# Which engine issues the loads of the context's raw weights: SyncE or GpSimd

## The chip, the cores and the metric

One core of one Trainium2 chip runs the whole program. The metric is the device time of one execution in microseconds (us). Below, PE is TensorE's matmuls, PEld its weight loads, DVE VectorE, ACT ScalarE, POOL GpSimd, SP SyncE; SPq and POOLq are the queues on which SP and POOL issue their DMAs.

## What is computed

Two transformer blocks, one after the other, on 256 tokens of width 1024, all in float32. The first has two attentions, a cross attention and a mixture of 32 experts (two chosen per token). The second is two layers deep and runs on two sequences: the tokens that leave the first block, and a context of 256 rows that depends on no token. The part that matters here is the context's, which in the first layer goes through an FFN, a mixer and another FFN, and in the second layer through one more FFN and a key and value projection:

```
mod = silu(c) @ ada_w + ada_b                    # 9 vectors of 1024 for each layer
h  = h + 0.5 * mod[2] * swiglu(modulate(h, mod[0], mod[1]), w_in, w_out)
swiglu(h) = (silu(g) * u) @ w_out,   g, u = split(h @ w_in),   hidden width 2816
```

All of the context's work can run beside the first block. Its result is needed only in the second layer's attention of the tokens.

## The kernel before

A float32 weight is read from DRAM as a "raw" tile and is split into two float32r parts: a high part, which ACT copies (`sph`), and a low part, raw minus high (`spl`). Each product is then three matmuls (high by high, high by low, low by high). `split` does this for pieces of 128 x 512.

There are two streams of work with buffers of their own, class `Stream`. `fore` (its tiles are named f...) has the first block, the experts and the tokens; its raw tiles are 128 x 2048 (1024 KB), five buffers. `back` (tiles b...) has the context; its raw tiles are 128 x 1024 (512 KB), five buffers, and three buffers each for `bsph` and `bspl`. In `back` the low part is subtracted by POOL (`LOW`, line 32: b=(1, 1)), in `fore` by DVE, with few exceptions.

- `load` (lines 182 to 185) takes a raw tile and issues its DMA on SP, for both streams. `pair` (187) calls it once for a wide tile and twice for a narrow one. The context's weights come through it: 132 tiles of `ffn_in`, 66 of `ffn_out`, 32 of the mixer (`e_sv`, `e_qk`, `e_u`, `e_v`, `e_o`, `e_out`) and 4 of `o_k` and `o_v`, 234 in all, and so 468 subtractions on POOL.
- `ada` (528) loads the modulation weights for `back` straight on SP, partly into the same raw buffers; PE reads those tiles itself. `narrow` (599) and the table of the spatial gate (1400 to 1402) also load on SP.
- `experts_in` and `experts_out` (1155 to 1184) load 24 wide tiles for each of 8 groups of experts, and multiply them directly, in float32, with no split.
- `squares` (264) adds squares of the residual, with POOL in two of its steps (278).
- `out_proj` (359), `ffn_steps` (419) and `even_steps` (1320) call these in turn.

Order: a planner lays out each engine's instructions once, when the program is built, by a priority that each stream works out from a due time (`SEG`, line 1797, and `priority`, 86): a start plus a slope times the matmul work that the stream has done. On the chip every engine then takes its instructions in that fixed order. `link` (157) adds edges for the planner: an instruction comes after the one before it of the same stream on the same engine key, and `self.after` can add one more edge. These edges are of the kind NoSync: they bind the planner's order, and put no wait into the program. The splits have a chain of their own (`S.side`, line 200), so the planner may put them anywhere between the loads of their engine.

At the loop for left-over experts (lines 1267 to 1274) the first stretch ends. Three of the six rounds of the context's last FFN are meant for before it (`PLAN`, -1: 'rrr'), three for after. Line 1912 says that the first SP instruction of the late rounds comes after `K.moe_load`, the last load of an expert weight.

Of the kernel before, what the change touches and what calls it, by code (L numbers as in the profile page):

```python
# [69 lines left out]
class Stream:  # L70
# [18 lines left out]
    def low(self, nc):  # L89

        self.lows += 1
        return nc.gpsimd if self.pool_low and self.lows % self.pool_low[1] < self.pool_low[0] else nc.vector

    def t(self, tag, shape, dt=F32):
        self.n += 1
        return self.pool.tile(shape, dt, tag=tag, bufs=self.bufs[tag], name=f"{self.name}{tag}{self.n}")
# [52 lines left out]
class Kern:  # L149
# [31 lines left out]

    def load(self, S, src):
        raw = S.t("raw", [128, S.unit])
        self.nc.sync.dma_start(raw, src)
        return raw

    def pair(self, S, src):
# [6 lines left out]
    def misc(self, S, tag, shape, src, dt=F32):  # L194
        t = S.t(tag, shape, dt)
        self.real.gpsimd.dma_start(t, src)
        return t
# [39 lines left out]
    def newton(self, S, src, n, scale, eps):  # L237
        nc = self.nc
        v, y, t = S.t("c", [128, n]), S.t("c", [128, n]), S.t("c", [128, n])
        nc.vector.tensor_scalar(v, src, scale, eps, op0=OP.mult, op1=OP.add)  # L240
        nc.vector.tensor_scalar(t.bitcast(I32), v.bitcast(I32), 1, None, op0=OP.arith_shift_right)
        nc.vector.tensor_scalar(y.bitcast(I32), t.bitcast(I32), -1.0, float(0x5F3759DF), op0=OP.mult, op1=OP.add)
        for _ in range(3):
            nc.vector.scalar_tensor_tensor(t, y, -0.5, y, op0=OP.mult, op1=OP.mult)
            nc.vector.tensor_tensor(t, t, v, op=OP.mult)
            nc.vector.scalar_tensor_tensor(y, t, 1.5, y, op0=OP.add, op1=OP.mult)
        return y
# [1554 lines left out]
def kernel(ctx: ExitStack, tc: tile.TileContext, I, out, dbg=None, stop=None):  # L1802
    K = Kern(tc, I, dbg)
    nc = K.nc
# [39 lines left out]
    def late(what):  # L1844
        c = K.cres
        for w in what:
            if w == "r":
                next(K.c1a)
            elif w == "a":
                m = K.nada  # L1850
                K.nada += 1
                for _ in K.ada(back, 1, range(m, m + 1), ("raw",)):
                    pass
            elif w == "k":
                assert next(K.c1a, None) is None and K.nada >= 5
                if dbg:
                    dbg("hc1a", c)
                K.odd_kv(back, K.modulated(back, c, 1, 3, 1))
# [49 lines left out]
    for i in range(PLAN_N):  # L1908
        if i in PLAN:
            K.cur, K.stream = back.chain, back  # L1910
            if i == 0:
                K.after["sync"] = K.moe_load
                back.seg(*SEG["c1a"])
            elif "tensor" in fore.chain:
                K.after["tensor"] = fore.chain["tensor"]
            late(PLAN[i])
        K.cur, K.stream = fore.chain, fore
        if i == 0:
            fore.seg(*SEG["tok"])
        next(steps, None)  # L1920
# [154 lines left out]
```

## Time and profile before

| | |
|---|---|
| median of 3 runs | 2590.99 us (2584.66 to 2596.36) |
| the profiled execution | 2586.39 us, of which the span of instructions is 2584.6 us |
| PE busy | 2391.1 us, 93% of the span |
| POOL busy | 732.7 us, 28% |
| DMA moved | 617.37 MB, 239 GB/s over the span |

The profile is one execution. Its share of busy time is a mean over unlike stages: the start (to some 236 us), the first block with the first pieces of the context (to 452), experts and context together (452 to 1232), experts alone (1232 to 1320), and the tokens (to the end, with the last context work between 1320 and 1765). The rows of the stages stand below. A matmul record that lasts longer than its share of PE's time overlaps its neighbours, so busy PE is read as "something was running".

### The profile page before, as it was taken

The page shows a single profiled execution, that of the slowest core. Times are in us where ns is not written, and L with a number is a line of the kernel's source. Part 1 is how long each engine was busy: PE and PEld are TensorE (multiplying, and loading weights), DVE is VectorE, ACT ScalarE, POOL GpSimd, SP SyncE. Part 2 cuts the span into 40 slices and gives each one's busy share as a digit, 9 for nine tenths or more (in the row PEclk, how much of TensorE's full clock was granted, in tenths as well). Part 3 has the DMA queues.
Part 4 walks back from the last instruction along what each step waited for, and adds up shares of the span by engine and source line. Part 5 has one row for each costly group of instructions (what it writes and reads, how often), then busy time and mean ns, then how long its engine had stood idle before and what let it go on. Part 6 is the DMA issues. An engine that isn't in the chain of part 4 may idle for free. (4 is left out here: it accounts for less than half of the span.)

```text
span 2584.6 us, 48422 instructions
## 1 busy us (share of the span) xinstructions
PE 2391.1 (93%) x19032; PEld 2066.7 (80%) x19032; DVE 1482.6 (57%) x3179; ACT 1185.6 (46%) x2342; POOL 732.7 (28%) x584
## 2 busy tenths in 40 slices
PE   6999998998988999999679999998999899889998
PEld 4767998786666888878259998988899899767998
DVE  6555767335434334252147676766767866677766
ACT  4433554334433433444035555545555555465554
POOL 1000145664524665756041004231000100424000
PEclk9999999999989999999789999998999999899999
DMA  9897543997989898988874554462455455355452
GB/s 375 298 338 266 178 139 109 377 353 280 388 303 347 341 347 302 367 322 339 330 299 169 188 188 136 173 209 83 156 187 181 151 190 182 112 199 196 172 188 98
DMA packets 115238, 617.37 MB, mean 239 GB/s; under 512 B 13232, under 2 KB 14704, under 8 KB 63936
## 3 DMA queue, kind: packets, MB, share of 16 engines
q1 hardware_dynamic: 113616, 610.20, 64.2%
q0 software_dynamic: 1392, 4.06, 0.5%
q8 instruction: 150, 2.46, 0.4%
q14 instruction: 80, 0.66, 0.1%
HBM read 612.11 MB, written 2.10 MB: 238 GB/s over the span
## 5 line engine op out<-in xcount | busy, mean ns | idle before, releaser
L58 POOL TENSOR_TENSOR bspl<-braw,bsph 128x512 fp32r<-128x512 f32 x468 | 611.2, 1315 | 885.9 <-ACT bsph L58 757.8
L58 ACT ACTIVATE fsph<-fraw 128x512 fp32r<-128x512 f32 x764 | 478.6, 628 | 518.7 <-PE fps L58 438.1
L58 DVE TENSOR_TENSOR fspl<-fraw,fsph 128x512 fp32r<-128x512 f32 x712 | 500.7, 706 | 288.7 <-ACT fsph L58 286.1
L58 PE MATMUL fps<-fxh,fspl 128*128 128x256 f32 (+1 forms) x2000 | 573.4, 287 | 3.5 <-POOL fspl L58 2.5
L58 PE MATMUL fps<-fxh,fsph 128*128 128x256 f32 (+1 forms) x2000 | 574.0, 287 | 2.7 <-ACT fxh L58 2.4
L58 PE MATMUL fps<-fxl,fsph 128*128 128x256 f32 (+1 forms) x2000 | 569.5, 285 | 7.3 <-DVE fxl L58 7.3
L58 ACT ACTIVATE bsph<-braw 128x512 fp32r<-128x512 f32 x468 | 290.7, 629 | 394.4 <-PE bps L58 323.4
L58 PEld LDWEIGHTS fps<-fxl,fsph 128*128 128x128 f32 x2000 | 382.6, 191 | 11.8 <-DVE fxl L58 11.1
L58 PEld LDWEIGHTS fps<-fxh,fsph 128*128 128x128 f32 x2000 | 382.8, 191 | 10.3 <-issue 4.6
L58 PEld LDWEIGHTS fps<-fxh,fspl 128*128 128x128 f32 x2000 | 381.6, 191 | 11.0 <-DVE fspl L58 4.8
L58 PE MATMUL bps<-bxh,bsph 128*128 128x256 f32 x1264 | 365.8, 289 | 10.8 <-ACT bsph L58 5.0
L58 PE MATMUL bps<-bxh,bspl 128*128 128x256 f32 x1264 | 366.4, 290 | 2.8 <-POOL bspl L58 2.3
L58 PE MATMUL bps<-bxl,bsph 128*128 128x256 f32 x1264 | 361.9, 286 | 0.9 <-DVE bxl L58 0.7
L58 PE MATMUL fps<-fk,fsph 128*128 128x256 f32 x1632 | 299.6, 284 | 2.2 <-ACT fk L58 1.5
L58 PEld LDWEIGHTS bps<-bxh,bsph 128*128 128x128 f32 x1264 | 245.4, 194 | 33.0 <-issue 10.2
L58 PEld LDWEIGHTS bps<-bxh,bspl 128*128 128x128 f32 x1264 | 245.4, 194 | 27.2 <-POOL bspl L58 17.7
L58 PEld LDWEIGHTS fps<-fk,fsph 128*128 128x128 f32 x1632 | 255.1, 192 | 7.0 <-DVE fk L58 3.4
L58 PEld LDWEIGHTS bps<-bxl,bsph 128*128 128x128 f32 x1264 | 245.2, 194 | 7.6 <-DVE bxl L58 4.0
L58 PE MATMUL fps<-fraw,fk 128*32 128x512 f32 (+1 forms) x1600 | 213.9, 651 | 37.0 <-DMA fraw<-in_w_eu_dram 20.3
L58 POOL TENSOR_TENSOR fk<-fk,fk 128x512 f32<-128x512 f32 x16 | 21.1, 1322 | 794.0 <-ACT fk L58 788.9
L58 PE MATMUL fps<-fk,fspl 128*128 128x256 f32 x816 | 231.7, 284 | 0.0
L58 DVE SCALAR_TENSOR_TENSOR bk<-bk,bps 128x256 f32<-128x256 f32 (+1 forms) x148 | 60.5, 411 | 250.9 <-ACT bk L58 249.0
(359 smaller groups left out, 3489.7 us busy)
## 6 DMA issues: line engine op xcount, KB each, us to landing
fraw<-in_ffn_in_dram SPq DMA_DIRECT2D x88, 1024.0 KB, 4.9
braw<-in_ffn_in_dram SPq DMA_DIRECT2D x132, 512.0 KB, 6.4
fraw<-in_w_eg_dram SPq DMA_DIRECT2D x66, 1024.0 KB, 7.4
fraw<-in_w_eu_dram SPq DMA_DIRECT2D x66, 1024.0 KB, 9.0
fraw<-in_w_ed_dram SPq DMA_DIRECT2D x66, 1024.0 KB, 7.4
fraw<-in_ffn_out_dram SPq DMA_DIRECT2D x44, 1024.0 KB, 4.9
braw<-in_ffn_out_dram SPq DMA_DIRECT2D x66, 512.0 KB, 5.9
braw<-in_ada_w_dram SPq DMA_DIRECT2D x59, 512.0 KB, 7.4
```

The source lines that it names most:

```text
L58: r = f(*args, **kw)
```

## The change

The loads that go through `load` are issued by POOL for the context's stream, and by SP as before for the other. The edge for the late rounds is hung on the first instruction of the key "gpsimd" instead of "sync", still after `K.moe_load`, which remains an instruction of SP. `ada`, `narrow` and the gate's table stay with SP. The loads of the context are now linked in one chain with the context's other POOL instructions that are not splits, the additions in `squares`.

```diff
+    def loader(self, nc):
+
+        return nc.gpsimd if self.name == "b" else nc.sync
...
     def load(self, S, src):
         raw = S.t("raw", [128, S.unit])
-        self.nc.sync.dma_start(raw, src)
+        S.loader(self.nc).dma_start(raw, src)
         return raw
...
             if i == 0:
-                K.after["sync"] = K.moe_load
+                K.after["gpsimd"] = K.moe_load
                 back.seg(*SEG["c1a"])
```

## Rows read from the trace of the kernel before

**Rows 1.** Page, part 1: busy time, share, instructions.
```profile
PE 2391.1 (93%) x19032; PEld 2066.7 (80%) x19032; DVE 1482.6 (57%) x3179; ACT 1185.6 (46%) x2342; POOL 732.7 (28%) x584
```

**Rows 2.** Stretch, us; busy us of PE, PEld, DVE, ACT, POOL; PEclk; DMA share; GB/s.
```profile
452.00:1232.00 780.00, 742.12 (x5797) 588.42 (x5796) 303.88 (x671) 312.87 (x599) 441.95 (x347) 0.97 0.89 339
1232.00:1320.00 88.00, 51.82 (x301) 15.18 (x300) 8.80 (x20) 4.93 (x9) 3.91 (x4) 0.75 0.90 344
...
646.00:711.00 65.00, 59.89 (x453) 43.87 (x446) 30.39 (x80) 28.77 (x60) 32.46 (x27) 1.00 0.98 387
```

**Rows 3.** PE by group, 1232 to 1320: busy, mean ns, idle before, releasers.
```profile
L58 PE MATMUL fps<-fraw,fk 128*32 128x512 f32 x240 | 44.1, 876 | 32.7 <-DMA fraw<-in_w_eu_dram 19.4 <-DMA fraw<-in_w_ed_dram 12.7 <-ACT fk L58 0.7
```

**Rows 4.** What SP's queue waited for, 452 to 1227.
```profile
SPq L58 <- POOL bspl L58: 404.5, 146, 12.3
SPq L58 <- PE fps L58: 204.3, 131, 9.9
```

**Rows 5.** What PE waited for, 452 to 1227: us, times, longest.
```profile
PE bps L58 <- POOL bspl L58: 4.2, 4, 1.6
...
PE fps L58 <- DMA fraw<-in_w_ed_dram: 1.3, 1, 1.3
...
PE fps L58 <- DMA fraw<-in_w_eu_dram: 0.9, 1, 0.9
```

**Rows 6.** DMA issues, 452 to 1227: count, KB each, median us to landing.
```profile
fraw<-in_w_eg_dram SPq DMA_DIRECT2D x56, 1024.0 KB, 7.4
...
braw<-in_ffn_in_dram SPq DMA_DIRECT2D x88, 512.0 KB, 6.7
braw<-in_ffn_out_dram SPq DMA_DIRECT2D x44, 512.0 KB, 6.7
```

**Rows 7.** Tile braw: duration ns, least, median, most.
```profile
L58 POOL TENSOR_TENSOR bspl<-braw,bsph x468: 1256/1292/2245, 236.6 to 1763.9; 128x512 fp32r<-128x512 f32 x156
L58 SPq DMA_DIRECT2D braw<-in_ffn_in_dram x132: 327/328/672, 222.2 to 1627.6; - x132
```

**Rows 8.** SP's instructions in order of time, end of the experts: start, us.
```profile
1218.85 20.09 SPq L58 DMA_DIRECT2D fraw<-in_w_ed_dram  x6
...
1288.48 18.08 SPq L58 DMA_DIRECT2D fraw<-in_w_ed_dram  x8
1306.61 17.21 SPq L58 DMA_DIRECT2D braw<-in_ffn_in_dram  x7
```

**Rows 9.** POOL by group, whole span: busy, mean ns, idle before.
```profile
L1387 POOL DMA_DIRECT2D dk<-bq x4 | 2.3, 566 | 15.4 <-DVE bq L58 11.5 <-DVE bc L58 3.9
...
L1711 POOL DMA_DIRECT2D cres<-in_ctx_dram x1 | 0.5, 533 | 0.0
```

**Rows 10.** POOL, then ACT, then PE in order of time, one burst.
```profile
1061.36 7.04 POOL L58 TENSOR_TENSOR bspl<-braw,bsph 128x512 fp32r<-128x512 f32 x5 [2.19 <-ACT bsph L58]
...
1062.10 0.63 ACT L58 ACTIVATE bsph<-braw 128x512 fp32r<-128x512 f32 x1 [0.82 <-PE bps L58]
1063.53 0.63 ACT L58 ACTIVATE bsph<-braw 128x512 fp32r<-128x512 f32 x1 [0.80 <-PE bps L58]
...
1066.61 1.93 PE L58 MATMUL fps<-fraw,fk 128*32 128x512 f32 x16
```

**Rows 11.** POOL in order of time: sums of squares in the mixer's projection.
```profile
806.41 1.29 POOL L58 TENSOR_TENSOR bk<-bk,bk 128x512 f32<-128x512 f32 x1
...
815.72 1.30 POOL L58 TENSOR_TENSOR bspl<-braw,bsph 128x512 fp32r<-128x512 f32 x1
```

**Rows 12.** Page, part 6: loads that POOL issues now, us to landing.
```profile
cres<-in_ctx_dram POOLq DMA_DIRECT2D x1, 1024.0 KB, 12.0
...
dv<-bk POOLq DMA_DIRECT2D x1, 512.0 KB, 8.3
```

**Rows 13.** PE in order of time, where the experts end.
```profile
1316.34 3.53 PE L58 MATMUL fps<-fraw,fk 128*32 128x512 f32 x16 [1.34 <-DMA fraw<-in_w_ed_dram]
1319.80 0.39 PE L58 MATMUL bps<-bxh,bsph 128*128 128x256 f32 x1
```

## The prediction, before the result was known

> **What bounds the kernel now.** I read the busy times of the page first, then the table of stretches, then the waits of PE, and only then those of SP. PE is busy for 2391 of 2584.6 us [rows 1], so all that any change can win is some 190 us, spread over stages that mostly have no context load in them. The table of stretches narrows this to two. From 452 to 1232, experts and context together, PE is busy for 742 of 780 us while DMA runs at 0.89 [rows 2]: both are nearly full, PE more so. From 1232 to 1320 the context has nothing left to do, PE is busy for 52 of 88 us at a granted clock of 0.75, and waits 32 us for expert weights [rows 2, 3]: a tail bound by DMA.
>
> The tempting view is the wait list of SP. From 452 to 1227 its queue stood 404 us waiting for POOL to finish with a raw tile of the context, 146 times [rows 4]. Those waits are what the change takes out of SP. They are not PE's: in the same stretch PE waited 2.2 us for expert weights and 4.2 us for a low part from POOL [rows 5]. And SP was not late for the experts: of the 166 expert loads of the stretch (56, 56 and 54 by the three weights [rows 6]) 131 found their own buffer still in use by PE when their turn came, and waited for that [rows 4]. At most the other 35 can have been held up by a context load ahead of them.
>
> **What the change removes.** 234 issues of 0.328 us leave SP [rows 7], 77 us on an engine that nothing waits for, and the 404 us of waiting with them. On the order of work as it stands, the gain is bounded by PE's waits for expert weights: 2.2 us in the shared stretch. The 32 us of the tail are not part of it: between SP's expert loads at 1218.85 and 1306.6 no context load was issued, the first comes at 1306.61 [rows 8]. So 0 to 2.2 us; I take 1 us.
>
> **What it adds to POOL.** Each of the 234 loads now takes POOL the time of an issue. POOL already issues a few loads, and one takes 0.566 us [rows 9]. That is 132 us in all, of which 164 (88, 44 and the mixer's 32) x 0.566 = 93 us fall between 452 and 1232, where POOL has 780 - 442 = 338 us idle [rows 2, 6]. The mean hides the rhythm, though. In a burst PE takes a new half tile every 1.43 us (1062.10 to 1063.53 on ACT), POOL subtracts five in 7.04 us with no gap worth the name, and rests 2.2 us while PE multiplies two expert tiles in 1.93 us [rows 10]. What covers an issue is the lead of the three split buffers. A buffer is free when PE is done with it; ACT takes 0.63 us to refill it, POOL 1.29 us (its median [rows 7]) and some 0.08 us of handover, 2.0 us in all; PE comes back to it after two other halves, 2.86 us. The lead is 0.86 us. A pair of halves with a load costs POOL 2 x 1.37 + 0.57 = 3.31 us against 2.86 us at which PE takes them, so each pair of a burst eats 0.45 us of lead: the first two pairs are covered, and a five-half burst ends about 0.05 us late, after which the 2.2 us give the lead back. With some 67 bursts (335 halves in the stretch by five) that is 3 us. Its bounds: 0 when the bursts are shorter, and 167 pairs x 0.45 = 75 us when there is no lead at all. Less than zero is excluded, since POOL only gets more to do. I take 4 us, near the end that the buffers support. The other 70 loads lie where POOL is busy for 733 - 442 = 291 of 1805 us [rows 1, 2], with 35 pairs of 0.45 us, 16 us, as their bound; I take 0.
>
> **Waits that move to POOL.** A load needs a raw tile whose last reader was, for nearly all, POOL's own subtraction; placed right behind it, it waits for nothing. Two cases differ. Where the tile was read by the matmuls of the modulation weights, POOL waits for PE; the only large block of these ends with the context's first loads, before POOL has its first subtraction at 236.6 [rows 7], so nobody stands behind it. And the additions of squares now share a chain with the loads: the last pair of loads in the mixer's projection must follow the addition at 806.4. They could start at 807.7, take 0.57 us to issue and some 6.7 us to land [rows 6], 815.0; their first subtraction ran at 815.72 [rows 11]. The same holds at the ends of the FFNs, where the first product of the next part waits for a norm anyway. Cost 0, and at most 8 us (one load's issue and landing) if a norm is shorter than I think; I take 0.
>
> **The landing.** From SP a 512 KB load lands in 6.7 us [rows 6]. From POOL I have 8.3 us for 512 KB in a busy stretch, 12.0 us for 1024 KB beside the initial loads [rows 12]. A tile is asked for four tiles ahead of its use, in bursts of 9.2 us for two and a half tiles that is 14.7 us, more than either. Cost 0.
>
> **The late loads.** The edge that holds the late rounds behind the last expert load was, on SP, also an order on the chip, since both stood in one queue. With the loads on POOL it binds the planner alone. POOL's next instruction after the last early subtraction is then a late load, so five loads can start near 1236 (POOL is busy for 3.9 us after 1232 [rows 2]) instead of 1306.6. They carry 5 x 0.524 MB = 2.6 MB, 7.6 us at 344 GB/s [rows 2], into a stretch bound by DMA; what they save behind it is little, since the context's first late matmul, at 1319.80, followed straight on the last expert one [rows 13]. Cost 0 to 7.6 us; DMA has a tenth free there, so I take 3 us.
>
> **The sum.** -1 + 4 + 0 + 0 + 3 = +6 us on the profiled execution's 2586.4 us, 2592 us. The median of the runs lies 4.6 us above that execution; I put half of that on top and forecast 2594 us, 0.1% above the median of before. About 0.5% (13 us, so 2578 to 2604 us) is what a measurement of this kernel can tell from no change.
>
> **The rivals.** The sum keeps the order of work. But the planner lays it out anew with the loads on another queue, and what it moves has a price that can be read. Between 1218.85 and 1306.6 SP issued 30 expert loads (six, eight, and between them sixteen of the other two weights), 2.93 us for each, bound by DMA; in the shared stretch one costs PE 1.93 / 2 = 0.97 us [rows 8, 10]. Moving one expert load is worth 2.0 us either way.
>
> First rival, faster: the experts get ahead. With SP for themselves their loads come earlier in the plan, and DMA has room for it: 0.98 in the best slice against 0.89 in the stretch [rows 2], 70 us or 24 loads. Half of that, 12 loads, gives -24 us, 2570 us; the end is the tail's own idle, 36 us, 2558 us. For it speaks the 404 us that SP stood still; against it that 131 of 166 loads waited for PE, not for SP.
>
> Second rival, slower: the context gets ahead. Its loads no longer stand in one line behind those of the experts, which are twice as long. If that lets the context run 12 loads earlier against the experts, the tail grows by as many: +24 us, 2618 us; 20 loads give 2634 us. It decides from the point where the context's last early subtraction ends more than 10 us before 1232 while the tail gets longer than 88 us. For it: the tail shows that the present order already favours the context. Against: PE, not DMA, sets the context's pace in the shared stretch.
>
> Third, slower by POOL: the lead is not there in long bursts or with uneven ones, and a third of the 75 us stays: +25 us, 2619 us.
>
> Fourth, slower by VectorE. A subtraction took 1.256 us at the least and 2.245 us at the most [rows 7], so something holds POOL by up to 0.99 us at times, though the median lies only 36 ns above the least. If one load in four of the 164 were held that long, with no cover, it would be +41 us, 2635 us. The Trainium skill ("SBUF — State Buffer", section "SBUF: two separate sides") speaks against this change outright: the descriptors of a DMA that GpSimd issues are written by GpSimd itself, and it can't write them while VectorE holds the port that the two share, so such DMAs should be issued from SP or ACT. No row shows it on a load here: the four issues within the stretch have a mean of 0.566 us, against 0.533 us for one at the quiet start [rows 9].
>
> That the change doesn't do what it says is not one of them: the loads leave SP by construction; the modulation loads stay there.
>
> **How the numbers follow.** The forecast (no change that can be told) 0.37; faster by the first rival 0.31; slower 0.32, of which the second has 0.19, the third 0.09 and the fourth 0.04. The range runs from 2560 to 2632 us: it leaves out the far end of the first rival, some 0.08, and the fourth with the far end of the second and the third, some 0.1. Cases of both signs hold much of it; the forecast's own range is 2580 to 2604 us.
>
> **What would show it.** In the profile after: SP's waits for POOL gone and those for PE about as before; 234 more POOL issues of some 0.57 us; PE's waits for a low part grown from 4.2 us by a few us (if by 20, the third rival). Issues that last over 1 us speak for the fourth. The length of the stretch in which only experts run tells the first rival (well under 88 us) from the second (well over). The forecast is wrong if that stretch changes by more than 15 us, however right the rest is.

## The result, and the profile after

The changed kernel is slower: 2616.2 us (median of 4 runs, 2607.2 to 2619.0) against 2590.3 us beside it, a ratio of 1.0104 with a 95% interval of 1.0081 to 1.0127. That is 26 us, where "no change" was forecast. The profiled execution took 2607.2 us, so its 2605.5 us of span show some 21 us of the 26.

The page of the changed kernel, part 1 [rows 1]:

```profile
PE 2394.7 (92%) x19032; PEld 2077.9 (80%) x19032; DVE 1509.6 (58%) x3179; ACT 1186.1 (46%) x2342; POOL 852.6 (33%) x818
```

POOL has its 234 instructions more and 120 us. What nobody asked for is VectorE: the same 3179 instructions take 27 us longer than the 1482.6 us of before. PE's idle time is 2605.5 - 2394.7 = 210.8 us against 193.5.

The two stretches of [rows 2] (same columns):

```profile
452.00:1232.00 780.00, 720.72 (x5519) 558.98 (x5521) 302.10 (x647) 295.36 (x566) 486.08 (x473) 0.95 0.87 336
1232.00:1320.00 88.00, 75.45 (x600) 56.51 (x592) 25.02 (x47) 26.61 (x48) 55.18 (x54) 0.90 0.93 355
```

PE did 278 matmuls fewer from 452 to 1232 us, and after it the context goes on beside the experts. Its last early matmul and the experts' last ones, from PE in order of time:

```profile
1295.94 0.28 PE L58 MATMUL bps<-bk,bspl 128*128 128x256 f32 x1
...
1327.80 1.92 PE L58 MATMUL fps<-fraw,fk 128*32 128x512 f32 x16 [2.31 <-DMA fraw<-in_w_ed_dram]
1329.65 0.39 PE L58 MATMUL bps<-bxh,bsph 128*128 128x256 f32 x1
```

The stretch in which only experts run lasts 34 us, where it was 88 [rows 2], and yet it ends 10 us later than in [rows 13]. So the planner did move the experts ahead of the context (by the two orders of PE, up to 538 of the context's 5172 early matmuls stand later against the experts' than before; the expectations below say 528), the tail shrank, and the time went up.

What SP's queue waited for, 452 to 1227 us (us in total, times, longest) [rows 4]:

```profile
SPq L58 <- PE fps L58: 554.8, 164, 22.0
...
SPq L58 <- POOL bspl L58: 5.4, 1, 5.4
```

The 404 us of waiting for POOL are gone, and SP now waits for PE instead, at 164 loads. What PE waited for in that stretch [rows 5]:

```profile
PE bps L58 <- DVE bk L58: 16.7, 10, 4.7
PE bps L58 <- ACT bk L58: 14.5, 13, 4.2
PE bps L58 <- POOL bspl L58: 6.0, 6, 1.9
PE fps L58 <- DVE bc L58: 4.9, 1, 4.9
...
PE fps L58 <- DMA fraw<-in_w_eu_dram: 3.1, 4, 1.1
```

Low parts from POOL cost 6.0 us where they cost 4.2: POOL does not feed PE much later. The long rows are VectorE's and ACT's. POOL's issues, whole span, by tile (ns: least, median, most) [rows 7, 9]:

```profile
L58 POOL TENSOR_TENSOR bspl<-braw,bsph x468: 1251/1290/2077, 233.7 to 1786.9; 128x512 fp32r<-128x512 f32 x156
L58 POOL DMA_DIRECT2D braw<-in_ffn_in_dram x132: 527/567/654, 218.1 to 1645.3; - x132
```

An issue takes 0.567 us as forecast, and none is stretched. The landings over the whole span (KB each, median us to landing; from SP it was 6.4 and 5.9 us):

```profile
braw<-in_ffn_in_dram POOLq DMA_DIRECT2D x132, 512.0 KB, 6.9
...
braw<-in_ffn_out_dram POOLq DMA_DIRECT2D x66, 512.0 KB, 5.7
```

In the window of [rows 6], 452 to 1227 us, `ffn_in` lands in 7.9 us where it landed in 6.7 (7.3 in e9 below, in the same order from SP), and the few loads of `e_qk` and `e_sv` in 12.8 and 13.6 us (9.7 and 6.5 in e9).

### The profile page after: what moved, and what is told of

It is laid out like the page before. It is cut to its first block, busy times and chain, and to the rows that moved or that the text cites. A ratio compares the mean times of both kernels' runs of the same rounds, so it can differ in the third digit from the quotient of the medians.

```text
span 2605.5 us, 48304 instructions
## 1 busy us (share of the span) xinstructions
PE 2394.7 (92%) x19032; PEld 2077.9 (80%) x19032; DVE 1509.6 (58%) x3179; ACT 1186.1 (46%) x2342; POOL 852.6 (33%) x818
## 3 DMA queue, kind: packets, MB, share of 16 engines
q0 software_dynamic: 35088, 126.76, 13.6%
## 5 line engine op out<-in xcount | busy, mean ns | idle before, releaser
L58 DVE TENSOR_TENSOR fspl<-fraw,fsph 128x512 fp32r<-128x512 f32 x712 | 506.1, 714 | 288.8 <-ACT fsph L58 286.2
L58 POOL TENSOR_TENSOR fk<-fk,fk 128x512 f32<-128x512 f32 x16 | 21.1, 1320 | 785.5 <-ACT fk L58 780.4
L58 PEld LDWEIGHTS bps<-bxh,bspl 128*128 128x128 f32 x1264 | 248.8, 197 | 35.6 <-issue 19.7
L58 PE MATMUL fps<-fraw,fk 128*32 128x512 f32 (+1 forms) x1600 | 204.6, 624 | 17.5 <-DMA fraw<-in_w_ed_dram 12.6
L58 PE MATMUL bps<-bk,bsph 128*128 128x256 f32 x1056 | 200.9, 289 | 3.2 <-DVE bk L58 1.7
```

The costliest lines, as they stand in the source:

```text
L58: r = f(*args, **kw)
```

## The experiments

Twelve kernels, each timed against the kernel before. In brief (time beside it 2588 to 2591 us; "VectorE" is its busy time in the one profiled execution, always for the same 3179 instructions):

| run | loads issued by | order | median us | ratio, 95% interval | VectorE us |
|---|---|---|---|---|---|
| kernel before | SP | its own | 2589 to 2591 | 1 | 1482.6 |
| changed | POOL | its own | 2616.2 | 1.0081 to 1.0127 | 1509.6 |
| e1 | POOL | PE as before | 2616.7 | 1.0083 to 1.0118 | 1527.2 |
| e2 | SP | PE as changed | 2588.1 | 0.9989 to 1.0013 | 1484.8 |
| e3 | POOL, own chain | its own | 2611.0 | 1.0058 to 1.0091 | 1490.9 |
| e4 | SP, and 234 small DMAs by POOL | PE as before | 2607.5 | 1.005 to 1.009 | 1531.0 |
| e5 | SP, and 234 small POOL operations | PE as before | 2614.8 | 1.0077 to 1.0116 | 1494.1 |
| e6 | POOL, own chain | PE as before | 2614.2 | 1.0073 to 1.0114 | 1535.7 |
| e7 | ACT, own chain | PE as before | 2607.6 | 1.0057 to 1.0101 | 1483.4 |
| e8 | POOL | all five engines as before | 2634.7 | 1.0167 to 1.0193 | 1530.1 |
| e9 | SP | all five engines as changed | 2591.2 | 0.9999 to 1.0026 | 1478.4 |
| e10 | POOL, own chain | all five as before | 2617.2 | 1.0085 to 1.0119 | 1534.2 |
| e11 | SP, and 234 small POOL operations | all five as before | 2616.3 | 1.0087 to 1.0122 | 1484.7 |
| e12 | ACT, own chain | all five as before | 2599.0 | 1.0018 to 1.0049 | 1479.9 |

**Is it the order?** The planner laid out everything anew, so the first question is whether the 26 us are the new order's or POOL's. An order can be held with edges for the planner alone: the sequence in which one kernel's engine goes from stream to stream is written down, and each first instruction of a run gets an edge to the last of the run before it. This is the code of e8 to e12; the runs that hold PE alone do the same for one engine.

```diff
+    def hold(self, part):
+        for key, text in ORDER.items():
...
+                if prev is not None:
+                    self.tc.add_manual_dep(
+                        these[0], prev.name,
+                        mybir.DependencyInfo(mybir.DependencyClass.NoSync, mybir.DependencyReason.DATA),
+                        reason="held order")
+                prev = these[-1]
```

e1, the changed kernel with PE's order of before:

> The loads are issued by POOL as in the changed kernel, but PE's instructions are held to the order that they have in the kernel before (edges for the planner alone, at each place where PE goes over from one stream to the other). Theory A, the new order: in the changed kernel PE's program has up to 528 of the context's 5172 early matmuls later against the experts' than before, so that the routing and the mixer have less other work beside them; the 26 us come from that. Then this kernel needs 2590 us, within 7 us of the kernel before. Theory B, POOL on the chip: issuing a load takes POOL 0.57 us, and with an issue between them its subtractions run without a break and hold up VectorE (a multiplication of 64 columns in the routing lasted 5.8 us); the order is innocent. Then this kernel needs 2609 to 2620 us, as the changed one. If both count, it lies between, and its distance from 2590 is POOL's part. In either case VectorE's longest instructions should stay as long as in the changed kernel, over 3 us.

e2, the kernel before with PE's order of the changed one:

> The other corner: the loads stay with SP as in the kernel before, and PE's instructions are held to the order that they have in the changed kernel. Theory A, the new order: 2610 to 2620 us, like the changed kernel, with the stretch of experts alone shortened as there. Theory B, POOL on the chip: 2585 to 2597 us, like the kernel before. In both no VectorE instruction should be held up for more than 1.5 us, since POOL issues no loads.

Theory A fell in both: 2616.7 and 2588.1 us. But with PE alone held, the planner still rearranged VectorE and ACT, so the two corners were made again with all five engines held (only the loads find their own places).

e8:

> The loads are issued by POOL, and now the order of all five engines is held to that of the kernel before (PE, VectorE, ACT, POOL's calculations, SP's other loads); only the 234 loads find their own places among POOL's calculations. Theory C, the planner after all: with PE's order alone held, VectorE's and ACT's were still laid out anew, and every such kernel but the one with SP's loads lost 19 to 27 us. Then this kernel needs 2586 to 2597 us. Theory D, POOL on the chip: the issues make the low parts late and hold up VectorE in any order. Then 2605 to 2617 us, and the delay against the kernel before grows at the same places as with PE's order alone: the routing (near 400 us), the end of the mixer's projection (812 us).

e9:

> The other corner once more, complete: the loads are issued by SP, and the order of all five engines is that of the changed kernel. Theory C, the planner: 2605 to 2617 us, like the changed kernel. Theory D, POOL on the chip: 2584 to 2596 us, like the kernel before and like the run with PE's order alone.

e9 needs 2591.2 us: the whole order of the changed kernel, with SP issuing, costs nothing that can be told. e8 needs 2634.7 us: the old order with POOL issuing is worse than either theory gave. So the new order isn't the cause; it is even the better of the two for POOL's loads, by 18 us. And the balance that the new order brings is worth nothing. PE's waits over the whole span, kernel before:

```profile
PE fps L58 <- DVE fk L58: 46.3, 26, 5.7
PE fps L58 <- DMA fraw<-in_w_eu_dram: 20.3, 8, 4.8
...
PE bps L58 <- DVE bk L58: 10.0, 7, 2.7
PE bps L58 <- ACT bk L58: 9.8, 10, 3.2
```

and e9:

```profile
PE fps L59 <- DVE fk L59: 58.9, 27, 6.4
PE bps L59 <- DVE bk L59: 15.5, 11, 4.7
PE bps L59 <- ACT bk L59: 14.3, 13, 4.1
...
PE fps L59 <- DMA fraw<-in_w_eu_dram: 6.3, 5, 3.5
```

The tail gives back 14.0 us of waiting for expert weights, and 12.6 + 5.5 + 4.5 = 22.6 us come on where PE waits for routing, norms and squares with less other work beside them.

**Where does POOL cost it?** Where two kernels have the same order, each matmul can be set against its counterpart, and the difference of their starts is the delay up to there. In us, by the time in the kernel that stands second (one execution each; much of what a column shows at 375 was there at 230 us, before POOL's first subtraction, so the growth from there is read; e11's execution is the slowest of its runs, 7 us above their median):

| at | 375 | 475 | 800 | 825 | 1100 | 1125 | 1225 | 1350 | 1800 |
|---|---|---|---|---|---|---|---|---|---|
| changed against e9 | -6.0 | -0.6 | 4.4 | 5.3 | 11.2 | 11.2 | 12.5 | 15.7 | 19.7 |
| e8 against before | 3.8 | 15.1 | 24.0 | 33.2 | 31.8 | 41.8 | 42.0 | 45.0 | 48.4 |
| e10 against before | 2.3 | 17.5 | 21.9 | 22.2 | 24.8 | 25.4 | 25.6 | 29.1 | 32.6 |
| e11 against before | 6.7 | 9.8 | 16.5 | 15.5 | 21.7 | 24.2 | 27.1 | 28.2 | 37.2 |
| e12 against before | 0.1 | 1.8 | 4.7 | 5.7 | 1.0 | 1.6 | 1.7 | 4.6 | 6.9 |

Little is lost after the context ends, some 1790 us (at most 3 us, in e12). Not all of the delay is waiting: of the 21.6 us between the spans of the changed kernel and e9, 15.0 are idle PE and 6.6 are busier PE; of e10's 32.6 us over the kernel before, 19.1 and 13.5. The granted clock has a part in that. From 375 to 475 us (columns of [rows 2]), in the kernel before and in e10:

```profile
375.00:475.00 100.00, 90.36 (x701) 80.50 (x701) 62.24 (x134) 43.03 (x87) 56.61 (x44) 0.95 0.49 172
```

```profile
375.00:475.00 100.00, 83.22 (x605) 75.71 (x602) 63.77 (x128) 39.61 (x81) 56.52 (x56) 0.88 0.36 116
```

In e10 PE did 96 matmuls fewer in these 100 us, and the clock stood at the lower of its two levels (1.2 instead of 2.4 GHz) for about 24 us, before for 10. The matmuls of this part of the program wait 9 us longer there and keep PE busy for 6 us longer.

This first step, 375 to 475, is the experts' routing: a chain of small VectorE operations, on which PE waits. VectorE there in the changed kernel, and then POOL (start, us):

```profile
409.59 0.22 DVE L58 TENSOR_REDUCE fc<-fk 128x2 f32<-128x64 f32 x1
409.84 5.83 DVE L58 TENSOR_TENSOR fk<-fk,fc 128x64 f32<-128x64 f32 x1
415.71 0.19 DVE L58 TENSOR_SCALAR fk<-fk 128x64 f32<-128x64 f32 x1
```

```profile
409.35 0.57 POOL L58 DMA_DIRECT2D braw<-in_ffn_in_dram  x1
409.94 3.79 POOL L58 TENSOR_TENSOR bspl<-braw,bsph 128x512 fp32r<-128x512 f32 x3
413.69 0.57 POOL L58 DMA_DIRECT2D braw<-in_ffn_in_dram  x1
414.28 1.30 POOL L58 TENSOR_TENSOR bspl<-braw,bsph 128x512 fp32r<-128x512 f32 x1
```

and in e9, in the same order, VectorE from the second of these on, and POOL:

```profile
413.46 1.01 DVE L59 TENSOR_TENSOR fk<-fk,fc 128x64 f32<-128x64 f32 x1
414.50 1.19 DVE L59 TENSOR_SCALAR fk<-fk 128x64 f32<-128x64 f32 x1
415.73 1.34 DVE L59 TENSOR_TENSOR fk<-fk,consts 128x64 f32<-128x64 f32 x1
```

```profile
410.58 6.40 POOL L59 TENSOR_TENSOR bspl<-braw,bsph 128x512 fp32r<-128x512 f32 x5
```

In e9 VectorE gets in after each subtraction, at up to 1.15 us of waiting apiece. In the changed kernel an operation of 64 columns stands from one issue on through three subtractions, the next issue and the fourth subtraction, and ends as that does. What it costs is less than the one line suggests, since e9 pays its smaller waits at several operations: this part of the chain (from the operation on 32 columns to `fk<-fk,consts`) takes from 408.21 to 416.16 us in the changed kernel, 7.95 us, and from 410.68 to 417.07 us in e9, 6.39 us. PE's wait for it, at 423.6 us, is 1.4 us longer than in e9; two more of its waits for VectorE, at 393.0 and 441.8 us, are longer by 1.9 and 1.2 us. These three make 4.5 of the 5.4 us by which the changed kernel's delay grows at the routing. The growth there is 5 to 15 us wherever POOL issues (changed, e8, e10; 7 us in e4) and 1.7 to 3.1 us in e11 and e12.

Taking a duration's excess over the shortest tenth of its form, no VectorE instruction of the kernel before or of e9 was held for over 1.15 us; in the changed kernel 18 were held for over 1.5 us, in e10 28. The Trainium skill ("SBUF — State Buffer", section "SBUF: two separate sides") has VectorE and GpSimd share a pair of ports under a lock that one of them keeps for a whole instruction; the waits of up to 1.15 us beside subtractions of 1.29 us agree with that. A wait through four subtractions, as above, does not follow from it.

**The shared chain.** e3, the changed kernel with the loads linked apart from the additions of squares:

```diff
+        self.loads = Eng(K, nc.gpsimd, "loads")
...
-        return nc.gpsimd if self.name == "b" else nc.sync
+        return nc.loads if self.name == "b" else nc.sync
...
-                K.after["gpsimd"] = K.moe_load
+                K.after["loads"] = K.moe_load
```

> The changed kernel, with POOL's loads linked in a chain of their own instead of in one chain with POOL's additions of squares. The planner's order of PE then has the context at most 324 matmuls behind the kernel before, against 528 in the changed one. Theory A, the new order: the loss shrinks about as the lag, 26 x 324 / 528 = 16 us, so 2606 us (2600 to 2612). Theory B, POOL on the chip: as many issues and subtractions as in the changed kernel, so 2610 to 2620 us.

2611.0 us: 5 us less than the changed kernel, with intervals that overlap. It lies within both theories' figures and decides nothing between them. The same in PE's old order, e6:

> POOL's loads in the old order of PE, with the loads in a chain of their own, apart from the additions of squares. In the run with one chain the delay against the kernel before grows by 8 us where the mixer's projection ends (at 812 us of the kernel before), where the next FFN's loads were issued behind an addition. If that place is due to the shared chain, this kernel is 6 to 9 us faster than that run: 2608 to 2611 us. If the place is late for another reason, 2614 to 2619 us.

2614.2 us, 2.5 us less than e1, which tells nothing by itself; in its trace the 8 us at 812 us are gone, and others came at other places, since VectorE and ACT were laid out anew. With all five engines held it is clear. e10:

> POOL's loads, the order of all five engines held to that of the kernel before, and the loads in a chain of their own instead of the one with the additions of squares. In the same kernel with the shared chain the delay grows by 7, 9 and 10 us where a part of the context ends (near 600, 812 and 1105 us of the kernel before): there four or five loads stand behind the last addition of squares and are issued in one go, and ACT waits 9 us for the first to land. If the shared chain is the cause there, these 26 us go: 2605 to 2612 us, and the routing keeps its 11 us. If the places are late for VectorE's sake, 2625 to 2637 us.

2617.2 us, 17.4 us less than e8, and between the two figures of the expectation. In the table e8 grows by 9.2 us from 800 to 825 and by 10.0 us from 1100 to 1125, and e10 by 0.3 and 0.6. What happens there in e8, POOL and then ACT:

```profile
1132.80 1.28 POOL L59 TENSOR_TENSOR bk<-bk,bk 128x512 f32<-128x512 f32 x1
1134.03 2.65 POOL L59 DMA_DIRECT2D braw<-in_ffn_in_dram  x5
```

```profile
1140.96 0.63 ACT L59 ACTIVATE bsph<-braw 128x512 fp32r<-128x512 f32 x1 [9.11 <-DMA braw<-in_ffn_in_dram]
```

Five loads of the next part stand behind the last addition of squares, and the landing of the first lies open. The expectation put 26 us on the chain; its part is 17 us in the old order, and in the changed kernel's some 5 us by e3, which is not clear of the noise and has a layout of its own. In the changed kernel's trace one such place shows, at the last pair of loads in the mixer's projection, POOL and then ACT:

```profile
844.12 1.29 POOL L58 TENSOR_TENSOR bk<-bk,bk 128x512 f32<-128x512 f32 x1
845.36 1.09 POOL L58 DMA_DIRECT2D braw<-in_e_out_dram  x2
```

```profile
854.30 1.15 ACT L58 ACTIVATE bsph<-braw 128x512 fp32r<-128x512 f32 x2 [2.74 <-DMA braw<-in_e_out_dram]
```

PE waits 3.1 us there at 855.0 us, and not at all at the same matmul in e9. The routing's step stays in e10, and is 15 us instead of e8's 11.

**Issue or time?** e4 leaves the weights to SP and lets POOL issue as many DMAs that carry nearly nothing:

```diff
+        if S.name == "b":
+            self.tiny += 1
+            self.nc.loads.dma_start(self.d_tiny[:, self.tiny], raw[:, :4])
```

> The kernel before, with its loads on SP and PE's instructions held to their order of before; POOL issues besides, for each of the 234 loads, one DMA of 16 bytes per partition out of the raw tile that has landed, into a spare piece of DRAM, in a chain of its own. So POOL issues as often as in the changed kernel (128 rows each), and no weight travels by its queue. If the loss comes from POOL's issuing (its 0.57 us, or VectorE held while issues and subtractions follow one another), this kernel loses most of the 27 us of the run with POOL's loads in the old order: 2605 to 2615 us, with VectorE instructions that are held for over 1.5 us. If it comes from the way of the data (landings from POOL's queue, transfers that start at other times) or from the chain with the squares, 2586 to 2595 us.

2607.5 us, with 25 VectorE instructions held for over 1.5 us: issues hold up VectorE without any weight in POOL's queue, and such a kernel loses some 19 us (the profiled execution, 2618.8 us, is the slowest of its runs). That the issues alone cost them is not shown, since e4 adds other waits: each small DMA on POOL waits until its tile has landed, SP stood 59 us at 21 loads until a small DMA had read the tile, and PE's waits for a low part grew from 5.1 to 17.8 us. e5 has a calculation instead of an issue:

```diff
-        S.low(self.nc).tensor_tensor(l, src, h.bitcast(F32), op=OP.subtract)
+        low = S.low(self.nc)
+        if S.name == "b" and S.lows % 2 == 0:
+            low.tensor_tensor(l[:, :208], src[:, :208], h[:, :208].bitcast(F32), op=OP.subtract)
+        low.tensor_tensor(l, src, h.bitcast(F32), op=OP.subtract)
```

> The kernel before with PE's order of before, in which POOL subtracts the first 208 columns of every second half tile twice: an extra operation of some 0.55 us for each load, as long as an issue, but a calculation. If POOL's time is what costs (each low part is late by what stands ahead of it), 2605 to 2615 us. If it is the issue itself that holds up VectorE, 2588 to 2597 us, and no VectorE instruction is held for more than 1.5 us.

2614.8 us, and so against the theory of the held VectorE; no instruction was held for over 1.2 us. e11 is the same with all five engines held, to have no doubt from a new layout:

> SP issues the loads, the order of all five engines is that of the kernel before, and POOL calculates the first 208 columns of every second half tile twice: 0.5 to 0.6 us more of work for each load, the length of an issue, and no issue. If the length is what costs, as much as in the run with POOL's loads in a chain of their own: 2605 to 2612 us. If it is the issue, behind which VectorE does not get in between two subtractions, 2588 to 2597 us, with no step at the routing.

2616.3 us, above its expectation's figure for the length. A calculation of (881.1 - 732.7) / 234 = 0.63 us for each load costs as much as the issues do. By the traces it goes another way, though. The page's part 1 of e11 and then of e10:

```profile
PE 2407.8 (92%) x19032; PEld 2076.8 (79%) x19032; DVE 1484.7 (57%) x3179; ACT 1185.7 (45%) x2342; POOL 881.1 (34%) x818
```

```profile
PE 2404.6 (92%) x19032; PEld 2077.0 (79%) x19032; DVE 1534.2 (59%) x3179; ACT 1185.0 (45%) x2342; POOL 850.7 (33%) x818
```

and PE's waits for a low part, whole span, in e11 and in e10:

```profile
PE bps L59 <- POOL bspl L59: 14.8, 26, 1.6
```

```profile
PE bps L59 <- POOL bspl L59: 5.2, 7, 1.6
```

The extra calculation stands ahead of a low part that PE needs next: 26 waits where the kernel before has 6, and VectorE's time is what it was. Of the 16.7 us by which PE is busier than before, 12 stand at the matmuls that read a low part (counted by how far each carries PE's end forward), so that these and the waits make 22 of the 36.9 us of this execution. The issue stands where there is room for it (5.2 us of such waits, before 5.1), and VectorE works 52 us longer; PE's waits for VectorE's results grow from 89.6 to 102.7 us, which is 13 of the 32.6 us. In the table e11 has 3 us at the routing, where e10 has 15. So POOL had no 0.6 us to give for a load in either way. In the real change VectorE's chain pays at the routing; for the rest that is argued. VectorE's busy time alone doesn't measure the loss: e3 loses 22 us with VectorE only 8 us above the kernel before.

**Any other engine?** e7 lets ACT issue the loads:

> As the run before it in this call, with the loads issued by ACT instead of POOL (a chain of their own, PE's order of the kernel before). If it is POOL's issuing that costs, and leaving SP is worth nothing, 2586 to 2595 us, with no VectorE instruction held for over 1.5 us. If any working engine loses as much, since the loads' waits for a free raw tile then stand in the way of its own work, 2605 us or more, with long waits of ACT's queue for POOL's low parts. If leaving SP is itself worth something, below 2583 us.

2607.6 us, with no VectorE instruction held for over 1.2 us: by its expectation, any working engine loses. With all five engines held, e12:

> ACT issues the loads, in a chain of their own; the order of all five engines is that of the kernel before, and POOL has no more to do than there. With PE's order alone held this lost 19 us. If that was the new layout of the other engines' work, 2586 to 2596 us: then leaving SP's queue is worth nothing and costs nothing. If a load in a working engine's queue costs by its time and its waits, 2600 to 2612 us. If SP's 404 us of waiting had held the experts' loads back, it would be faster than the kernel before by over 7 us.

2599.0 us, 8 us or 0.34% above the kernel before (0.18 to 0.49%), between two of the figures named. So most of e7's 19 us were the new layout. What is left is small, and it is a loss: taking the loads out of SP's queue gives nothing even where POOL and VectorE are left alone. VectorE's 1479.9 us are those of before. Between e10 and e12, in the same order, POOL as the issuer costs 18 us more than ACT.

## Why the prediction was right or wrong

**What can be won: right.** The argument that SP's 404 us were nobody's loss held. They went, SP waited for PE instead, and with ACT as the issuer nothing was won (8 us were lost). PE's waits for expert weights in the shared stretch were 2.2 us and are 3.1 us.

**POOL's issue, +4 us: the step that failed.** Its parts were right: 0.567 us each, 234 of them, none stretched, and PE's waits for low parts grew from 4.2 to 6.0 us, "a few". From that the sum took 4 us. Against e9, in the same order, the changed kernel has 15.0 us more of idle PE (210.8 to 2583.9 - 2388.1 = 195.8), and by the lists of PE's waits 8.2 of them are for VectorE's results, 5.8 for ACT's and 2.8 for POOL's, with 3.3 less for transfers. The runs put the term at 22 to 26 us (e3, e10: all that POOL's loads cost without the shared chain), not 4. Two things were wrong in it. The lead of the split buffers, worked out to some 0.05 us, was asked only how late a low part reaches PE; the term had nothing for VectorE, whose operations POOL holds up. And the lead doesn't cover what it was said to cover: in e11, where 0.63 us stand before every second half tile, as in the sum's own rhythm, the loss is 25 us and not 3 to 4. The 16 us set as the bound for loads outside the shared stretch and then taken as 0 belong to the same mistake: the routing (375 to 475), most of it ahead of 452, is the largest single step of e10. That the issues of the real change show in so few waits for low parts is a matter of where the planner put them, which the sum didn't work out.

**VectorE and POOL: the right pair, the wrong way round.** The fourth rival asked whether VectorE would hold up POOL's issues; its sign, issues of over 1 us, is absent (654 ns at the most). POOL held up VectorE. The rows of before could not tell it: a POOL that subtracts without a gap [rows 10] holds no VectorE instruction for over 1.15 us, in the kernel before or in e9.

**The chain with the squares, 0 and at most 8 us: mis-sized.** One place was looked at, with one pair of loads behind the addition; in the changed kernel PE waits 3.1 us at the last pair in the mixer's projection, for the landing of these loads (about 9 us from the issue at 845.4, not 6.7). There are several such places, with up to five loads, and in the old order they cost 17 us; in the changed kernel some 5, not clear of the noise.

**Landing 0 and late loads +3 us: not contradicted.** The 8.3 us of [rows 12] are no load's: `dv` lies in DRAM, so that row is a store. From 452 to 1227 us a load of `ffn_in` lands in 7.9 us from POOL and 7.3 from SP in the same order, both under the 14.7 us of cover; in the changed kernel ACT waits for a landing in that stretch only for the mixer's loads, 6.2 us in all, 4.2 of them for those behind an addition. The late loads began at 1293.8 us, not near 1236, since in the new order the context had work until 1296. Where the experts end, the delay against e9 grows from 12.5 us (at 1275) to 18.6 (1300) and falls to some 15 (1326); which part of the 3 us left is the late loads' isn't shown.

**The rivals and the stretch.** The first rival's mechanism came in full, the experts-only stretch fell from 88 to 34 us, and its 24 us did not: e9 has that order without POOL's issues and needs 2591 us. The price of 2.0 us for each expert load moved was read from the tail alone; what the moved load leaves behind, a short chain with less work beside it, has a price too. By its own test (the stretch changes by more than 15 us) the forecast was wrong; what made it so was another thing. Slower had 0.32, and 2616 us lies within the range of 2560 to 2632 us, beside the 2618 and 2619 us of the second and third rivals. That is luck: the second's tail got shorter instead of longer, the third's waits for low parts did not come, and POOL holding up VectorE has no term in the range.

**What stays open.** Shown are that the loads on POOL cost the time and the order doesn't, and VectorE's share at the routing. How the rest, 15 us in e10 and 20 in the changed kernel, divides between VectorE held, work that is late for ACT and PE behind it, and a lower clock is not: the steps are of 1 to 3 us. Of the 8 us that e12 loses, 3 us come from 1225 to 1350, at the experts' end: ACT issued five late loads there from 1299.0 us on, ahead of the last expert load at 1309.7, where SP issued them behind it before; that they cost the 3 us is not shown. Loads on POOL everywhere but in the routing weren't tried, since nothing is won by them elsewhere: no version here beats the kernel before.

## What to carry to other kernels

A queue that stands still costs nothing while the engine that bounds the kernel does not wait for it; look there first. An engine that has room by its busy share (POOL was at 28%) may have none to give: here 0.6 us more for each load cost about as much as a calculation as it did as an issue, and issues held up another engine's short operations. Before giving an engine issues, list the short chains beside it and who waits for them. And where a planner lays out the program anew, hold the order with planning edges and run both orders with both variants: four runs tell the edit from its layout.

## What was not expected of the hardware

With POOL's DMA issues between its subtractions, a VectorE operation of 64 columns lasted 5.83 us, and three of 256 columns 4.4 to 4.5 us, where beside subtractions alone, in the kernel before and in e9, none lost more than 1.15 us. It did not get in at the issues either: the one at 409.84 us waited through the issue at 413.69. Why VectorE comes in between two subtractions, and not behind an issue, no run here tells.

The subtractions by which VectorE makes the low parts of gate times up in the context's three FFNs show it over the whole span; VectorE by form (busy us, mean ns, idle before) in the changed kernel and in e9:

```profile
L58 DVE TENSOR_TENSOR bk<-bk,bk 128x256 fp32r<-128x256 f32 x66 | 69.6, 1054 | 31.5 <-ACT bk L58 31.4
```

```profile
L59 DVE TENSOR_TENSOR bk<-bk,bk 128x256 fp32r<-128x256 f32 x66 | 55.0, 834 | 30.7 <-ACT bk L59 30.6
```

The same 66 subtractions of 256 columns take 1054 instead of 834 ns each.
